# Tensor sums and low parts moved from the Pool engine to VectorE in the last three stages of a decoder block

## The chip, the cores and the metric

One core of a Trainium2 chip runs the whole kernel. Its engines work side by side, each through its own list of instructions in order: TensorE (PE in the views) multiplies matrices, VectorE (DVE) and the Pool engine (POOL, GpSimd) do elementwise work, ScalarE (ACT) copies, casts and activations, and SyncE (SP) issues the DMAs. The metric is the device time of one execution, in microseconds, as the median over runs.

## The reference, cut to what matters

A decoder block on 1024 tokens (1152 rows with padding and meta tokens), width 1024, everything float32. Two attention branches are merged, projected and added to the residual; a SwiGLU feed-forward of width D_FF = 2816 follows:

```
mixed = gate_a * (o_a @ w_branch_a) + gate_b * (o_b @ w_branch_b)
h = h + mixed @ w_out                                  # 1024 x 1024 by 1024 x 1024
hn = rms_norm(h, ffn_norm_g)
h = h + (silu(hn @ w_ffn_gate) * (hn @ w_ffn_up)) @ w_ffn_down
y = rms_norm(h, final_norm_g)
```

## The kernel before, in words

**Products of float32 values in two parts.** Each operand is split into a high part, a rounded copy that ScalarE makes, and a low part, the difference of the raw value and the high one, which VectorE or POOL subtracts. A product is three matmuls: high by high, low by high, high by low (`mm3`, whose instructions stand at L193). So for every operand tile of 128 x 512 there is one cast, one subtraction ("the low") and then matmuls that wait for both.

**Seven products for eight.** The output projection, the feed-forward products and the down projection are Winograd's form of Strassen's method: a 2 x 2 block product takes the seven products m1 to m7, whose operands are blocks or sums of blocks: s1 to s4 of one side, t1 to t4 of the other. In the output projection and the down projection they come in the orders m1 m5 m6 m3 m2 m7 m4 and m1 m5 m6 m3 m7 m2 m4. Between a product and the next, an elementwise engine makes the sums in place.

**Three stages matter here.**

- The *output projection* (`winograd`, called by `phase_mix`). X is the merged attention output, W is `w_out`, four tiles of 128 x 512 for each block. x sums (L1188) and x lows (L133, tile `fhl`) are VectorE's; w sums (L1188 too) and w lows (L131, tile `tl`) are POOL's. `NTH = 5` buffers hold w parts. Where a product ends, VectorE adds it to `h1` (L1218); when a block of 128 tokens is whole, `row_scale` (L1240 to L1246, chains of 128 x 1 instructions), ScalarE's scaling `xs` (L1255), eight transposes (L1264) and the gain (L1267, tile `hb`) make the normed, transposed operand B.
- The *first feed-forward pair*. `phase_ffn` makes the sums t1 to t4 of B in four cuts of 128 tokens (L1289 to L1292, tiles `bt` and `hb`): POOL has t1 and t2 of the first cut and every t3 and t4, VectorE the others. `operand` (L1318, L1319) splits each of the seven operands of B once, in four tiles: three lows on VectorE, the fourth on POOL. `ffn_hidden(ap, q)` runs for q = 0 to 10, each q a pair of 128-column slices of D_FF; `weight` takes the gate and up weights' high part on ScalarE (L1360) and low part on POOL (L1361). Only q = 0 waits for the operands of B to be made; the later ones find them ready.
- The *down projection* (`ffn_down`). For each product there are eleven k steps of one activation tile `da` and one weight tile `wd`. The activation's low is VectorE's, the weight's low is POOL's (both L1432, tiles `fhl` and `yhl`; in the last product `xl` and `yl`); the sum of weight tiles (L1462 in m5, L1464 in m6, L1466 in m7, L1468 in m4) is POOL's where k is odd and VectorE's where it is even.

**What sets the order.** A list scheduler with a model of the engines puts each engine's instructions in order when the program is built; the code's order decides only where that model is indifferent. Within an engine the order then is fixed: an instruction that waits holds all behind it.

Of the kernel before, what the change touches and what calls it, by code (L numbers as in the profile page):

```python
# [7 lines left out]
F32 = mybir.dt.float32  # L8
# [95 lines left out]
class Program:  # L104
# [1028 lines left out]
    def phase_mix(self):  # L1133
        nc, I = self.nc, self.I

        self.act_dram = {nm: [self.dr.tile([P, 512], F32, name=f"act{nm}_{k}") for k in range(NF // 2)]
                         for nm in ("11", "12", "22", "s1", "s2", "s3", "s4")}
        self.h1_dram = [self.dr.tile([P, D], F32, name=f"h1_dram{b}") for b in range(NB)]
        self.f_es, mes = ExitStack(), ExitStack()
        self.B, self.xs = {}, {}  # L1140
        self.fwp = self.f_es.enter_context(self.pool("fwp"))
        xp = mes.enter_context(self.pool("mixed"))

        X, W = self.X, self.W = [{ij: xp.tile([P, 4, 512], F32, name=f"{nm}{ij}") for ij in ("11", "12", "21", "22")} for nm in "xw"]
# [12 lines left out]
        for b in range(NB):
            with self.tc.issue_after(self.mixed_in):
                nc.sync.dma_start(self.h1[:, b, :], I["x"][0][P * b:P * b + P, :])
        self.rp = mes.enter_context(self.pool("ring", side="right"))  # L1160

        def done(b, nh):
            self.squares(b, nh)
            if nh == 0:
                nc.sync.dma_start(self.h1_dram[b], self.h1[:, b, :])
                self.norm_scaled(b)
                self.pending.append(b)
                if len(self.pending) > 1:
                    self.norm_transposed(self.pending.pop(0))

        self.pending = []
        banks = lambda name: [(self.sp if name in ("m2", "m5") else self.mm).tile(
            [P, 512], F32, name="s" if name in ("m2", "m5") else "ps", tag="s" if name in ("m2", "m5") else "ps") for _ in range(4)]
        self.winograd(X, W, 4, ("m1", "m5", "m6", "m3", "m2", "m7", "m4"), banks, nc.vector, nc.gpsimd, done)
        while self.pending:
            self.norm_transposed(self.pending.pop(0))
        mes.close()

    def winograd(self, a, b, kc, order, banks, seng, teng, done=None):

        nc = self.nc
        a, b, sums = dict(a), dict(b), {}

        def combine(eng, d, name, dst, x, y, op):
            for k in range(kc):
                eng.tensor_tensor(d[dst][:, k], d[x][:, k], d[y][:, k], op=op)  # L1188
            d[name] = d[dst]

        sub, plus = ALU.subtract, ALU.add
        for at, name in enumerate(order):
            if name == "m5":
                combine(seng, a, "s1", "21", "21", "22", plus)
                combine(teng, b, "t1", "12", "12", "11", sub)
            elif name == "m6":
                combine(seng, a, "s2", "s1", "s1", "11", sub)
                combine(teng, b, "t2", "t1", "22", "t1", sub)
            elif name == "m3":
                combine(seng, a, "s3", "11", "22", "s2", sub)  # L1200
                combine(teng, b, "t3", "11", "t2", "11", sub)
                combine(seng, a, "s4", "s2", "12", "s2", sub)
                combine(teng, b, "t4", "t2", "t2", "21", sub)
            an, bn, old, to = WINOGRAD[name]
            ps4 = sums[name] = sums[old] if old else banks(name)
            ops = []
            rows = name == "m4" and done
            for k in range(kc):
                ops.append((self.parts(a[an][:, k], self.fwp, ("fhl",), 4, False), self.parts(b[bn][:, k], self.rp, ("th", "tl"), NTH, True)))
            for k, i in [(k, i) for i in range(4) for k in range(kc)] if rows else [(k, i) for k in range(kc) for i in range(4)]:  # L1210
                c = slice(P * i, P * i + P)
                x, y = ops[k]
                self.mm3(ps4[i], [(x[0][:, c], x[1][:, c], *y)], start=not old and k == 0, stop=k == kc - 1, skip_group_check=bool(old))
                if k < kc - 1:
                    continue
# [54 lines left out]
    def phase_ffn(self):  # L1270
# [14 lines left out]
        B["t3"] = B["12"]  # L1285
        for at, n in CUTS:
            cut = {nm: B[nm][:, :, at:at + n] for nm in B}
            e = nc.gpsimd if at < 128 else nc.vector
            e.tensor_sub(cut["t1"], cut["12"], cut["11"])  # L1289
            e.tensor_sub(cut["t2"], cut["22"], cut["t1"])  # L1290
            nc.gpsimd.tensor_sub(cut["t3"], cut["22"], cut["12"])
            nc.gpsimd.tensor_sub(cut["t4"], cut["21"], cut["t2"])  # L1292
        self.tp2 = tp
        self.ring = es.enter_context(self.pool("dring"))
        with self.pool("act") as ap:
# [14 lines left out]
    def operand(self, name):  # L1310

        nc, hi = self.nc, self.Bhi[name]
        if name not in self.Blo:
# [2 lines left out]
            lo = self.Blo[name] = pool.tile([P, 4, 512], F32R, name=f"l{name}", tag=tag, bufs=1)  # L1316
            for k in range(4):
                nc.scalar.copy(hi[:, k], raw[:, k])  # L1318
                (nc.gpsimd if k == 3 else nc.vector).tensor_sub(lo[:, k], raw[:, k], hi[:, k].bitcast(F32))  # L1319
        return hi, self.Blo[name]  # L1320

    def parts(self, src, ring, tags, bufs, lo_pool):
# [9 lines left out]
    def ffn_hidden(self, ap, q):  # L1332
# [12 lines left out]
        def weight(a, name):  # L1345
# [74 lines left out]
    def ffn_down(self):  # L1420
# [6 lines left out]
        homes = {"11": ("h11", "h21", "b11"), "12": ("ht2", "b21", "ht1"), "22": ("bt2", "ht3", "bt1"), "21": ("h22", "b12", "ht4")}  # L1427
        rings, turn = ("bt4", "spare"), 0

        def split(src, hi, lo, pool):  # L1430
            nc.scalar.copy(hi, src)  # L1431
            (nc.gpsimd if pool else nc.vector).tensor_sub(lo, src, hi.bitcast(F32))  # L1432

        sums, gain = {}, None
        for name in ("m1", "m5", "m6", "m3", "m7", "m2", "m4"):
# [8 lines left out]
            for g, (k0, n) in enumerate(groups):  # L1444
# [8 lines left out]
                for i in range(n):  # L1453
# [3 lines left out]
                    if fresh:  # L1457
                        r, c = P * (2 * k + int(fresh[0]) - 1), 512 * (int(fresh[1]) - 1)
                        dma = nc.sync.dma_start(b[fresh][k], wd[r:r + P, c:c + 512])
                    e = nc.gpsimd if k % 2 else nc.vector  # L1460
                    if name == "m5":
                        e.tensor_sub(b["12"][k], b["12"][k], b["11"][k])  # L1462
                    elif name == "m6":
# [86 lines left out]
```

## Time and profile before

| | us |
|---|---|
| median of 3 runs | 1518.8 (1517.16 to 1520.61) |
| the profiled execution: time | 1516.53 |
| its span on the core | 1514.8 |
| TensorE busy, share of the span | 1398.1 (92%) |
| VectorE busy | 1009.9 (67%) |
| POOL busy | 914.7 (60%) |
| ScalarE busy | 817.0 (54%) |

The profiled execution has 1.7 us around its span and is 2.3 us under the median. Times in the views count from the start of the span. The output projection runs from about 744 to 832 us, the first feed-forward pair to about 913, the other ten pairs to about 1280, the down projection and the final norm to the end. Windows of the trace give busy time per engine in such a stretch; the timeline gives single instructions with the idle time in front and what ended it; the chain of waits is followed back from the last instruction.

### The profile page before, as it was taken

What the parts mean: (1) busy time and instruction counts of PE and PEld (TensorE: products, weight loads), DVE (VectorE), ACT (ScalarE), POOL (GpSimd) and SP (SyncE); (2) the same over time, 40 slices, a digit from 0 to 9 for tenths busy, and PEclk for the clock granted to TensorE, in tenths of its full rate; (3) what the DMA queues carried; (4) which work ended last, traced back from release to release, by engine and by line L of the source; (5) the groups of instructions that cost most, each with busy time, mean ns of one, the idle gap of its engine ahead of it and who ended that gap; (6) DMA issues with size and microseconds to landing.
All of it is one profiled execution on the core that took longest, in us unless ns stands there. A gap on an engine that the chain in (4) does not pass through costs nothing.

```text
span 1514.8 us, 21375 instructions
## 1 busy us (share of the span) xinstructions
PE 1398.1 (92%) x6847; PEld 1160.4 (77%) x6847; DVE 1009.9 (67%) x1950; ACT 817.0 (54%) x1743; POOL 914.7 (60%) x995
## 2 busy tenths in 40 slices
PE   4999697898898899999989699999999999999997
PEld 4988685677677688888768478888888888878876
DVE  7268997135686887785798984444444446697576
ACT  6347585983787777885336533333333334434463
POOL 4147465667665657664794675555555557596575
PEclk9999898999899899999999699999999999999999
DMA  6421121246444755337812023332232239723332
GB/s 207 133 77 29 29 71 49 91 138 198 125 138 126 182 147 162 125 102 236 308 54 94 18 97 126 106 109 96 100 104 97 99 105 317 295 70 121 115 105 111
DMA packets 148038, 189.79 MB, mean 125 GB/s; under 512 B 11331, under 2 KB 95126, under 8 KB 147670
## 3 DMA queue, kind: packets, MB, share of 16 engines
q1 hardware_dynamic: 147568, 188.28, 38.6%
q8 instruction: 54, 0.88, 0.2%
q14 instruction: 58, 0.48, 0.1%
q10 hardware_dynamic: 198, 0.14, 0.0%
q0 software_dynamic: 160, 0.01, 0.0%
HBM read 133.49 MB, written 58.03 MB: 126 GB/s over the span
## 4 chain that ended last, share of the span: by engine, by line
PE 60%; DVE 15%; POOL 7%; issue 7%; ACT 6%; DMA 6%; SPq 1%; POOLq 0%; ACTq 0%; DVEq 0%
PE ps L193 24%; PE s L193 20%; PE gps L193 8%; DVE mask L815 4%; ACT mask L857 2%; PE pv L1049 2%; PE s L1007 2%; PE tp L1038 2%; DMA kraw<-bk_dram 1%; DMA ga<-gate_dram 1%; POOL yhl L1432 1%; POOL y L1511 1%; PE tp L198 1%; PE pv L193 1%; DVE fhl L1432 1%
## 5 line engine op out<-in xcount | busy, mean ns | idle before, releaser
L1361 POOL TENSOR_TENSOR fhl<-fs,fhl 128x512 fp32r<-128x512 f32 x88 | 120.7, 1394 | 98.1 <-ACT fhl L1360 98.1
L1361 POOL TENSOR_TENSOR fhl<-fr,fhl 128x512 fp32r<-128x512 f32 x66 | 105.6, 1621 | 84.4 <-ACT fhl L1360 72.6
L188 POOL TENSOR_TENSOR w_lo<-w_raw,w_hi 128x512 fp32r<-128x512 f32 x60 | 82.4, 1375 | 90.5 <-ACT w_hi L187 76.3
L1432 POOL TENSOR_TENSOR yhl<-wd,yhl 128x512 fp32r<-128x512 f32 x66 | 96.5, 1468 | 55.2 <-ACT yhl L1431 53.6
L193 PE MATMUL s<-ht,fhl 128*128 128x512 f32 x384 | 123.4, 396 | 2.0 <-ACT fhl L1360 2.0
L1432 DVE TENSOR_TENSOR fhl<-da,fhl 128x512 fp32r<-128x512 f32 x66 | 89.2, 1365 | 47.0 <-ACT fhl L1431 46.8
L193 PE MATMUL ps<-ht,fhl 128*128 128x512 f32 x320 | 101.1, 392 | 0.0
L193 PE MATMUL gps<-oh,w_hi 128*128 128x512 f32 x232 | 94.6, 408 | 6.7 <-ACT gt L914 6.1
L857 ACT ACTIVATE mask<-high,smallg 128x784 bf16<-128x784 uint16 (+3 forms) x66 | 70.4, 1067 | 45.9 <-POOL smallg L866 28.1
L193 PE MATMUL s<-yhl,fhl 128*128 128x512 f32 x396 | 92.6, 392 | 2.5 <-POOL yhl L1432 2.3
L865 POOL TENSOR_SCALAR smallg<-smallg 128x1 f32<-128x1 f32 x128 | 58.8, 462 | 59.8 <-ACT mask L857 59.3
L193 PE MATMUL ps<-yhl,fhl 128*128 128x512 f32 x396 | 92.1, 391 | 1.5 <-DVE fhl L1432 1.5
L193 PE MATMUL gps<-ol,w_hi 128*128 128x512 f32 x232 | 93.4, 403 | 0.0
L193 PE MATMUL gps<-oh,w_lo 128*128 128x512 f32 x232 | 92.6, 399 | 0.0
L1431 ACT CAST yhl<-wd 128x512 fp32r<-128x512 f32 x66 | 41.0, 621 | 95.0 <-PE ps L193 43.2
L193 PEld LDWEIGHTS s<-yhl,fhl 128*128 128x128 f32 x396 | 74.0, 188 | 20.3 <-POOL yhl L1432 4.5
L193 PEld LDWEIGHTS ps<-yhl,fhl 128*128 128x128 f32 x396 | 74.0, 188 | 18.9 <-DVE fhl L1432 3.1
L193 PE MATMUL s<-h,fhl 128*128 128x512 f32 x272 | 88.2, 395 | 0.0
L193 PE MATMUL ps<-h,fhl 128*128 128x512 f32 x256 | 84.8, 403 | 3.6 <-ACT h L1318 3.6
L193 PEld LDWEIGHTS s<-ht,fhl 128*128 128x128 f32 x384 | 72.8, 190 | 19.4 <-ACT fhl L1360 2.8
L133 DVE TENSOR_TENSOR ptl<-tp,pth 128x512 fp32r<-128x512 f32 (+2 forms) x112 | 70.9, 645 | 24.2 <-ACT pth L127 22.9
L1360 ACT CAST fhl<-fr 128x512 fp32r<-128x512 f32 x66 | 39.7, 619 | 73.9 <-issue 33.3
(486 smaller groups left out, 4459.5 us busy)
## 6 DMA issues: line engine op xcount, KB each, us to landing
fr<-in_w_ffn_gate SPq DMA_DIRECT2D x22, 512.0 KB, 4.0
fr<-in_w_ffn_up SPq DMA_DIRECT2D x22, 512.0 KB, 4.7
wd<-in_w_ffn_down SPq DMA_DIRECT2D x44, 256.0 KB, 5.1
da<-acts SPq DMA_DIRECT2D x44, 256.0 KB, 3.9
w_raw<-in_w_in SPq DMA_DIRECT2D x40, 256.0 KB, 3.1
act<-a SPq DMA_DIRECT2D x33, 256.0 KB, 2.1
da<-act SPq DMA_DIRECT2D x33, 256.0 KB, 3.0
acts<-s SPq DMA_DIRECT2D x33, 256.0 KB, 2.0
```

Of the source, the lines that this page charges most:

```text
L133: nc.vector.tensor_sub(lo, ps, hi.bitcast(F32))
L188: (nc.vector if lo_dve else nc.gpsimd).tensor_sub(t[1], t[2], t[0].bitcast(F32))
L193: mm = self.nc.tensor.matmul(*args, **kw)
L815: nc.vector.tensor_scalar(self.mask[j], src[j], at[:, i:i + 1], None, op0=op, op1=ALU.add, accum_out=out[:, i:i + 1])
L857: nc.scalar.activation(self.mask[j], src[j], AF.Sign, bias=at[:, i:i + 1], scale=scale, accum_out=out[:, i:i + 1])
L865: g.tensor_scalar(c[:, o], acc[:, o], bar[:, o], b[:, o], op0=ALU.is_ge, op1=ALU.subtract)
L1007: nc.tensor.matmul(ps[:, :n], q[k][:, h, qc:qc + P], kb[:, h, at:at + n], start=k == 0, stop=k == 1)
L1038: mm = nc.tensor.transpose(pt[:, P * i:P * i + P], prs[par, e][:, NM + P * rr:NM + P * rr + P], self.ident)
L1360: nc.scalar.copy(hi, a[name])
L1361: nc.gpsimd.tensor_sub(lo, a[name], hi.bitcast(F32))
L1431: nc.scalar.copy(hi, src)
L1432: (nc.gpsimd if pool else nc.vector).tensor_sub(lo, src, hi.bitcast(F32))
```

## The change

The diff takes POOL out of 172 subtractions and sums: 28 w lows and 16 w sums of the output projection, the ten sums of B's cuts that POOL had, the fourth low of each of the seven operands, the 14 weight lows of q = 0, and in the down projection 77 weight lows and 20 weight sums. All go to VectorE in the same shape. POOL keeps the 140 weight lows of q = 1 to 10 and its work in the final norm. No cast, matmul or DMA is added or removed.

```diff
-        self.winograd(X, W, 4, ("m1", "m5", "m6", "m3", "m2", "m7", "m4"), banks, nc.vector, nc.gpsimd, done)
+        self.winograd(X, W, 4, ("m1", "m5", "m6", "m3", "m2", "m7", "m4"), banks, done)
...
-        def combine(eng, d, name, dst, x, y, op):
+        def combine(d, name, dst, x, y, op):
             for k in range(kc):
-                eng.tensor_tensor(d[dst][:, k], d[x][:, k], d[y][:, k], op=op)
+                nc.vector.tensor_tensor(d[dst][:, k], d[x][:, k], d[y][:, k], op=op)
             d[name] = d[dst]
...
             if name == "m5":
-                combine(seng, a, "s1", "21", "21", "22", plus)
-                combine(teng, b, "t1", "12", "12", "11", sub)
+                combine(a, "s1", "21", "21", "22", plus)
+                combine(b, "t1", "12", "12", "11", sub)
...
-                ops.append((self.parts(a[an][:, k], self.fwp, ("fhl",), 4, False), self.parts(b[bn][:, k], self.rp, ("th", "tl"), NTH, True)))
+                ops.append((self.parts(a[an][:, k], self.fwp, ("fhl",), 4, False), self.parts(b[bn][:, k], self.rp, ("th", "tl"), NTH, False)))
...
-            e = nc.gpsimd if at < 128 else nc.vector
-            e.tensor_sub(cut["t1"], cut["12"], cut["11"])
-            e.tensor_sub(cut["t2"], cut["22"], cut["t1"])
-            nc.gpsimd.tensor_sub(cut["t3"], cut["22"], cut["12"])
-            nc.gpsimd.tensor_sub(cut["t4"], cut["21"], cut["t2"])
+            nc.vector.tensor_sub(cut["t1"], cut["12"], cut["11"])
+            nc.vector.tensor_sub(cut["t2"], cut["22"], cut["t1"])
+            nc.vector.tensor_sub(cut["t3"], cut["22"], cut["12"])
+            nc.vector.tensor_sub(cut["t4"], cut["21"], cut["t2"])
...
-                (nc.gpsimd if k == 3 else nc.vector).tensor_sub(lo[:, k], raw[:, k], hi[:, k].bitcast(F32))
+                nc.vector.tensor_sub(lo[:, k], raw[:, k], hi[:, k].bitcast(F32))
...
-            nc.gpsimd.tensor_sub(lo, a[name], hi.bitcast(F32))
+            (nc.gpsimd if q else nc.vector).tensor_sub(lo, a[name], hi.bitcast(F32))
...
-            (nc.gpsimd if pool else nc.vector).tensor_sub(lo, src, hi.bitcast(F32))
+            nc.vector.tensor_sub(lo, src, hi.bitcast(F32))
...
-                    e = nc.gpsimd if k % 2 else nc.vector
+                    e = nc.vector
```

The new engine also changes what the scheduler puts beside what. From L1289 on, the changed file's line numbers are one lower.

VectorE, where the output projection goes over to m5, in the kernel before: x lows (`fhl`), sums of the x blocks (`x_8542` and `x_8540` are the blocks 21 and 11).

```order
L1188 TENSOR_TENSOR x_8542<-x_8542,x_8543 128x512
L133 TENSOR_TENSOR fhl<-x_8542,fhl 128x512
L1188 TENSOR_TENSOR x_8542<-x_8542,x_8540 128x512
L1188 TENSOR_TENSOR x_8540<-x_8543,x_8542 128x512
L133 TENSOR_TENSOR fhl<-x_8542,fhl 128x512
```

The same place in the changed kernel, from the last merge (L1117) on; `tl` are the w lows, `w_8545` and `w_8544` w blocks.

```order
L1117 TENSOR_TENSOR x_8542<-gt,ga 128x512
L1188 TENSOR_TENSOR x_8542<-x_8542,x_8543 128x512
L133 TENSOR_TENSOR tl<-w_8544,th 128x512 x4
L133 TENSOR_TENSOR tl<-w_8545,th 128x512
L1188 TENSOR_TENSOR w_8545<-w_8547,w_8545 128x512
L1188 TENSOR_TENSOR w_8544<-w_8545,w_8544 128x512
L133 TENSOR_TENSOR fhl<-x_8542,fhl 128x512
L133 TENSOR_TENSOR tl<-w_8545,th 128x512
L1188 TENSOR_TENSOR x_8542<-x_8542,x_8540 128x512
L1188 TENSOR_TENSOR w_8545<-w_8547,w_8545 128x512
L1188 TENSOR_TENSOR x_8540<-x_8543,x_8542 128x512
L1188 TENSOR_TENSOR w_8544<-w_8545,w_8544 128x512
```

Each k step of VectorE's list has grown from three instructions to six, and the first four w lows stand behind the last merge.

VectorE, where the sums of B's cuts (`bt`, `hb` of L1289 and L1290) lead to the first operands that need them, in the kernel before; L1267 is the gain on the transposed norm.

```order
L1289 TENSOR_TENSOR bt_9649<-hb_8781,hb_8779 128x4x128
L1267 TENSOR_TENSOR hb_8782<-s,vec 128x4x128
L1289 TENSOR_TENSOR bt_9649<-hb_8781,hb_8779 128x4x128
L1290 TENSOR_TENSOR bt_9650<-hb_8782,bt_9649 128x4x128 x2
L1319 TENSOR_TENSOR l_9742<-hb_8780,h_9653 128x512 x3
L1357 TENSOR_TENSOR fs<-fr,fs 128x512
```

And in the changed kernel, where L1288 to L1291 are t1 to t4, L1318 is the operand's low and L1360 a weight low:

```order
L1267 TENSOR_TENSOR hb_8782<-s,vec 128x4x128
L1290 TENSOR_TENSOR hb_8781<-hb_8782,hb_8781 128x4x128
L1288 TENSOR_TENSOR bt_9649<-hb_8781,hb_8779 128x4x128 x2
L1291 TENSOR_TENSOR bt_9651<-hb_8780,bt_9650 128x4x128
L1360 TENSOR_TENSOR fhl<-fs,fhl 128x512
L1289 TENSOR_TENSOR bt_9650<-hb_8782,bt_9649 128x4x128
L1290 TENSOR_TENSOR hb_8781<-hb_8782,hb_8781 128x4x128
L1289 TENSOR_TENSOR bt_9650<-hb_8782,bt_9649 128x4x128
L1290 TENSOR_TENSOR hb_8781<-hb_8782,hb_8781 128x4x128
L1318 TENSOR_TENSOR l_9742<-hb_8780,h_9653 128x512 x4
```

Between the last gain and the operand's lows there are now nine instructions of VectorE where there were three, and four lows where there were three.

VectorE in the down projection, before, at m5 beside the sums that m6 will want (`wd` the weight tiles, `fhl<-da` the activation lows):

```order
L1466 TENSOR_TENSOR wd_1_12858<-wd_1_13104,wd_1_12858 128x512
L1432 TENSOR_TENSOR fhl<-da,fhl 128x512 x2
L1464 TENSOR_TENSOR wd_2_13142<-wd_2_13383,wd_2_13142 128x512
L1466 TENSOR_TENSOR wd_2_12892<-wd_2_13142,wd_2_12892 128x512
L1432 TENSOR_TENSOR fhl<-da,fhl 128x512 x2
```

And after:

```order
L1431 TENSOR_TENSOR fhl<-da,fhl 128x512
L1465 TENSOR_TENSOR wd_0_12824<-wd_0_13066,wd_0_12824 128x512
L1463 TENSOR_TENSOR wd_1_13104<-wd_1_13345,wd_1_13104 128x512
L1431 TENSOR_TENSOR yhl<-wd_1_13104,yhl 128x512
L1431 TENSOR_TENSOR fhl<-da,fhl 128x512
L1465 TENSOR_TENSOR wd_1_12858<-wd_1_13104,wd_1_12858 128x512
```

Each k step is now four instructions on VectorE (L1463, two lows, L1465); before, VectorE had four for two steps, and POOL did the other four beside it.

## Rows read from the trace of the kernel before

**Rows 1.** The page: busy time of each engine over the span, and the shares of the chain that ended last.

```profile
PE 1398.1 (92%) x6847; PEld 1160.4 (77%) x6847; DVE 1009.9 (67%) x1950; ACT 817.0 (54%) x1743; POOL 914.7 (60%) x995
...
PE 60%; DVE 15%; POOL 7%; issue 7%; ACT 6%; DMA 6%; SPq 1%; POOLq 0%; ACTq 0%; DVEq 0%
```

**Rows 2.** Windows: start and end, length, then busy time and number of instructions of PE, PEld, DVE, ACT and POOL, the granted clock of TensorE, the DMA share and GB/s.

```profile
743.60:784.00 40.40, 35.68 (x148) 27.18 (x147) 39.44 (x33) 14.31 (x26) 40.33 (x24) 1.00 0.48 176
784.00:832.10 48.10, 47.76 (x221) 38.57 (x221) 41.85 (x91) 28.20 (x61) 26.05 (x18) 1.00 0.16 66
832.10:857.90 25.80, 15.69 (x60) 11.88 (x58) 25.59 (x51) 13.36 (x23) 16.34 (x13) 0.67 0.10 42
857.90:884.00 26.10, 20.14 (x73) 15.36 (x73) 23.36 (x21) 15.25 (x29) 20.04 (x13) 0.87 0.07 23
884.00:912.80 28.80, 28.80 (x118) 23.40 (x119) 23.55 (x24) 9.66 (x18) 19.43 (x13) 0.94 0.38 127
912.80:1280.00 367.20, 367.20 (x1600) 300.23 (x1599) 178.59 (x210) 129.27 (x233) 201.67 (x139) 1.00 0.36 122
1280.00:1318.00 38.00, 38.00 (x168) 31.07 (x167) 23.79 (x26) 15.42 (x27) 19.05 (x14) 1.00 0.94 344
1318.00:1350.60 32.60, 31.66 (x134) 24.51 (x133) 32.46 (x24) 12.56 (x22) 32.22 (x20) 1.00 0.19 62
1350.60:1383.50 32.90, 31.35 (x134) 24.37 (x132) 32.11 (x26) 12.56 (x22) 27.94 (x18) 1.00 0.35 116
1383.50:1443.40 59.90, 59.90 (x266) 49.64 (x265) 33.20 (x32) 27.47 (x52) 30.09 (x23) 1.00 0.31 106
1443.40:1467.00 23.60, 22.04 (x98) 17.94 (x97) 16.68 (x20) 17.68 (x36) 18.15 (x13) 1.00 0.24 79
```

**Rows 3.** The timeline of PE around the output projection's start and the first feed-forward pair: start, length, what, and in brackets the idle time in front and what ended it.

```profile
743.59 1.09 PE L193 MATMUL ps<-th,fhl 128*128 128x512 f32 x4
745.51 0.51 PE L193 MATMUL ps<-tl,fhl 128*128 128x512 f32 x1 [0.83 <-POOL tl L131]
...
832.12 0.39 PE L193 MATMUL ps<-th,fhl 128*128 128x512 f32 x1
836.09 1.22 PE L193 MATMUL ps<-h,fhl 128*128 128x512 f32 x2 [3.58 <-ACT h L1318]
840.35 1.97 PE L1264 MATMUL s<-ident,xs 128*128 128x128 f32 x8 [3.04 <-ACT xs L1255]
...
860.82 0.79 PE L193 MATMUL ps<-l,fhl 128*128 128x512 f32 x1 [2.94 <-DVE l L1319]
...
883.99 0.80 PE L193 MATMUL s<-ht,fhl 128*128 128x512 f32 x1 [0.89 <-ACT fhl L1360]
```

**Rows 4.** The timeline of VectorE at the end of the last feed-forward pair, with POOL at rest.

```profile
1286.79 0.69 DVE L1411 TENSOR_TENSOR s<-a,a 128x512 f32<-128x512 f32 x1
1287.51 0.69 DVE L1412 TENSOR_TENSOR s<-s,a 128x512 f32<-128x512 f32 x1
1288.12 0.68 DVE L1413 TENSOR_TENSOR a<-a,a 128x512 f32<-128x512 f32 x1
1288.72 0.69 DVE L1432 TENSOR_TENSOR fhl<-da,fhl 128x512 fp32r<-128x512 f32 x1
```

**Rows 5.** The timeline of POOL in the down projection's m1, with VectorE at rest beside it.

```profile
1299.89 1.30 POOL L1432 TENSOR_TENSOR yhl<-wd,yhl 128x512 fp32r<-128x512 f32 x1 [1.47 <-ACT yhl L1431]
```

**Rows 6.** The timeline of all engines in the down projection's m5.

```profile
1329.96 1.79 DVE L1464 TENSOR_TENSOR wd<-wd,wd 128x512 f32<-128x512 f32 x1
...
1331.29 1.63 POOL L1464 TENSOR_TENSOR wd<-wd,wd 128x512 f32<-128x512 f32 x1
1331.79 1.68 DVE L1466 TENSOR_TENSOR wd<-wd,wd 128x512 f32<-128x512 f32 x1
...
1332.88 1.75 POOL L1432 TENSOR_TENSOR yhl<-wd,yhl 128x512 fp32r<-128x512 f32 x1
```

**Rows 7.** The timeline of all engines at the end of the output projection, where the norm's small instructions meet POOL's weight lows of q = 0.

```profile
831.34 3.74 POOL L1361 TENSOR_TENSOR fhl<-fr,fhl 128x512 fp32r<-128x512 f32 x3 [11.85 <-DVE rh L1245]
831.35 1.30 DVE L1246 SCALAR_TENSOR_TENSOR rh<-rh 128x1 f32<-128x1 f32 x1
...
832.57 2.52 DVE L1245 SCALAR_TENSOR_TENSOR rh<-rh 128x1 f32<-128x1 f32 x2
...
835.02 0.15 DVE L1246 SCALAR_TENSOR_TENSOR rh<-rh 128x1 f32<-128x1 f32 x1
```

**Rows 8.** Groups of POOL's instructions from 740 to 1515 us, shapes kept apart: count, then busy time and mean ns of one, idle time in front and what ended it.

```profile
L1432 POOL TENSOR_TENSOR yhl<-wd,yhl 128x512 fp32r<-128x512 f32 x66 | 96.5, 1468 | 55.2 <-ACT yhl L1431 53.6 <-DMA wd<-in_w_ffn_down 1.4
L131 POOL TENSOR_TENSOR tl<-w,th 128x512 fp32r<-128x512 f32 x28 | 45.9, 1656 | 14.9 <-ACT th L127 10.2 <-PE tp L193 4.7
```

**Rows 9.** The chain of waits from 1316 to 1334 us, by line.

```profile
by line: POOL yhl L1432 44.6%; POOL wd L1464 27.1%; issue 27.1%; POOL wd L1466 11.0%; POOLq L1432 0.2%; POOLq L1464 0.1%
```

**Rows 10.** The timeline of VectorE at the start of the output projection.

```profile
744.96 1.05 DVE L1117 TENSOR_TENSOR x<-gt,ga 128x512 f32<-128x512 f32 x1
746.04 1.67 DVE L1188 TENSOR_TENSOR x<-x,x 128x512 f32<-128x512 f32 x1
```

**Rows 11.** Windows around the first feed-forward pair's idle stretches; the columns are those of rows 2.

```profile
836.10:853.10 17.00, 10.49 (x38) 8.29 (x39) 16.79 (x42) 6.70 (x9) 8.84 (x8) 0.50 0.08 31
860.00:866.80 6.80, 5.98 (x14) 4.73 (x15) 5.85 (x4) 5.66 (x11) 6.72 (x5) 0.50 0.01 2
```

More of the change, by code (lines that the diff above doesn't have):

```diff
@@ L1177, in phase_mix, with winograd @@
         mes.close()
-    def winograd(self, a, b, kc, order, banks, seng, teng, done=None):
+    def winograd(self, a, b, kc, order, banks, done=None):
         nc = self.nc
         a, b, sums = dict(a), dict(b), {}
-        def combine(eng, d, name, dst, x, y, op):
+        def combine(d, name, dst, x, y, op):
             for k in range(kc):
-                eng.tensor_tensor(d[dst][:, k], d[x][:, k], d[y][:, k], op=op)
+                nc.vector.tensor_tensor(d[dst][:, k], d[x][:, k], d[y][:, k], op=op)
             d[name] = d[dst]
@@ L1193, in winograd @@
             if name == "m5":
-                combine(seng, a, "s1", "21", "21", "22", plus)
-                combine(teng, b, "t1", "12", "12", "11", sub)
+                combine(a, "s1", "21", "21", "22", plus)
+                combine(b, "t1", "12", "12", "11", sub)
             elif name == "m6":
-                combine(seng, a, "s2", "s1", "s1", "11", sub)
-                combine(teng, b, "t2", "t1", "22", "t1", sub)
+                combine(a, "s2", "s1", "s1", "11", sub)
+                combine(b, "t2", "t1", "22", "t1", sub)
             elif name == "m3":
[L1200 to L1203, printed above, removed]
+                combine(a, "s3", "11", "22", "s2", sub)
+                combine(b, "t3", "11", "t2", "11", sub)
+                combine(a, "s4", "s2", "12", "s2", sub)
+                combine(b, "t4", "t2", "t2", "21", sub)
             an, bn, old, to = WINOGRAD[name]
@@ L1428, in ffn_down, with split @@
         rings, turn = ("bt4", "spare"), 0
-        def split(src, hi, lo, pool):
+        def split(src, hi, lo):
             nc.scalar.copy(hi, src)
-            (nc.gpsimd if pool else nc.vector).tensor_sub(lo, src, hi.bitcast(F32))
+            nc.vector.tensor_sub(lo, src, hi.bitcast(F32))
         sums, gain = {}, None
@@ L1475, in ffn_down @@
                         op = t[:, 0], t[:, 1], u[:, 0], u[:, 1]
-                    split(x, *op[:2], False)
-                    split(y, *op[2:], True)
+                    split(x, *op[:2])
+                    split(y, *op[2:])
                     ops.append(op)
```

## The prediction

> **What bounds the kernel now.** I first read the page: TensorE is busy for 92% of the span and holds 60% of the chain that ended last, so a change on VectorE and POOL can win only where TensorE stands still; VectorE has 15% of that chain and POOL 7% [rows 1]. Then the windows, to find those places. The rate without gaps is 59.90 us for 266 matmuls in 1383.5 to 1443.4, 0.225 us each [rows 2]. Against it:
>
> - start of the output projection, 743.6 to 784.0: 148 matmuls need 33.3 us and took 40.4, so 7.1 are lost; POOL is busy for 40.33 of these 40.4 and VectorE for 39.44;
> - end of the output projection to the third product of the first feed-forward pair, 832.1 to 884.0: 133 instructions of TensorE in 51.9 us, with VectorE busy for 25.59 + 23.36 = 48.95;
> - down projection: m5 (1318.0 to 1350.6) 134 x 0.225 = 30.2 of 32.6, lost 2.4; m6 (to 1383.5) 30.2 of 32.9, lost 2.7; m2 (1443.4 to 1467.0) 98 x 0.225 = 22.1 of 23.6, lost 1.5; together 6.6.
>
> From 912.8 to 1318.0 TensorE is busy all the time (367.20 of 367.20, 38.00 of 38.00) [rows 2].
>
> The PE timeline says who is late: POOL's `tl` at 745.51, after the output projection ScalarE's casts and `xs` (836.09, 840.35), which stand behind VectorE's norm, VectorE's `l` at 860.82 [rows 3]. In m5 the chain is POOL: 44.6% lows, 27.1% and 11.0% weight sums [rows 9].
>
> The timeline of VectorE and POOL then gives the reason. VectorE alone takes 0.68 us for a 128x512 subtraction of two SBUF tiles, and where one does not need the result before it the next starts 0.60 later (1287.51 to 1288.12, 1288.12 to 1288.72); where it does, 0.72 (1286.79 to 1287.51) [rows 4]. POOL alone takes 1.30 [rows 5]. When both work, each takes 1.63 to 1.79, and the starts on either engine lie 1.6 to 1.8 apart [rows 6]: a pair costs about 1.70, and two on VectorE alone would cost 1.20. POOL's help is worth less than nothing there. Even a 128x1 instruction of the norm takes 1.30 or 1.26 beside POOL (831.35, 832.57 for two) and 0.15 without it (835.02) [rows 7].
>
> **The change part by part.** It takes 172 instructions from POOL, whose mean is 1468 ns for `yhl` and 1656 ns for `tl` [rows 8], and gives 172 to VectorE; at 0.60 these are 103 us more. What decides is VectorE's pitch p in a mixed queue. Its bounds are 0.60 and 0.72 [rows 4]; I take 0.63, near the lower end, since the order puts other instructions between a sum and the low made from it, and a twentieth for the few that stand in a row. No cast, matmul or DMA is added.
>
> *A, start of the output projection.* The first w low, which POOL had made by 745.5, now stands behind the last merge (744.96) and a sum [rows 10, 3]. At 0.6 to 0.7 each VectorE comes to it at 746.3, and TensorE to the first `tl` at 746.9, 1.4 later than before. From there TensorE needs 144 matmuls x 0.225 = 32.4, to 779.3. VectorE has 52 instructions up to the first x low of m3: 31.2 us at 0.60 (777.5), 32.8 at 0.63 (779.0), 37.4 at 0.72 (783.7). TensorE sets the end in the first two. m3 began at 784.0: gain 4.7, 4.7 or 0.3. A w low now waits for its cast on VectorE, and behind it stand x sums and the `h1` additions that free PSUM banks. ScalarE is busy for only 14.31 of the 40.4 us [rows 2], so I cost that at nothing; were the casts late, POOL's 10.2 us of waiting for them [rows 8] would be the ceiling.
>
> *B, norm and first pair.* m3 to the end is bound by TensorE (47.76 of 48.10 [rows 2]) and moves along. Of the 32 transposes, 16 now stand behind m4's matmuls, which end some 1.8 us earlier for it (16 x 0.11; eight take 1.97 at half clock in rows 3, so half of that at the full one). m4 ends at 832.1 - 4.7 - 1.8 = 825.6. From there to the third product VectorE has 74 tile instructions and 35 small ones at some 0.13: 49.0 us at 0.60, 51.2 at 0.63, 57.9 at 0.72 (there from 830.0). The third product starts at 874.6, 876.8 or 887.9 instead of 884.0: gain of A and B together 9.4, 7.2 or -3.9. That VectorE takes 14 weight lows and 17 sums and operand lows here is why B gives little beyond A. What is late next is still VectorE. Afterwards TensorE is the bound as before, and POOL's 140 later lows are unchanged: 912.8 to 1280 moves as a block.
>
> *C, down projection.* In m5 VectorE has 48 instructions: 22 lows, 22 sums (those of m5 and m6) and 4 additions to `h1`. That is 28.8 us at 0.60, 30.2 at 0.63, 34.6 at 0.72, against 132 x 0.225 = 29.7 of TensorE. So m5 loses nothing, 0.6, or 4.4 to 4.9 (some 2 more than before); m6 and m2, with fewer sums left, lose nothing. Gain 6.6, 6.0 or 2.2. POOL was busy for 32.22 of 32.6 in m5 [rows 2]; its queue is now empty. m1 is bound by TensorE with the DMA engines at 0.94 [rows 2] and only moves; a weight sum that waits for its DMA now holds VectorE's other work, which I put at 0 to 2 us and take at 0, as TensorE had no gap there.
>
> Sum: -16.0 at 0.60, -13.2 at 0.63, +1.7 at 0.72. The profiled execution took 1516.53, so it would be 1503.3; the median lies 2.3 above, and 1518.8 - 13.2 = 1505.6 us.
>
> **The rivals.**
>
> *Each instruction waits until the one before is through.* Then p is 0.68, the duration itself [rows 4]. A: 52 x 0.68 = 35.4, to 781.7, gain 2.3. B: from 828.0, 74 x 0.68 + 4.6 = 54.9, to 882.9, gain of both 1.1. C: 48 x 0.68 = 32.6 in m5, as before; m6 and m2 give 4.2. Together -5.3: 1513.5. For it: dependent pairs do show 0.72. Against it: the starts 0.60 apart in rows 4. The Trainium skill, page "VectorE: DVE Perf Modes", section "The DRAIN you can't avoid", says this as a rule: the next operation doesn't start until the pipeline is empty, though it adds that one not held starts earlier. By that rule the time would be the 1513.5; the trace of rows 4 shows the exception as the common case.
>
> *Slower: VectorE becomes the bound.* One in-order queue for x lows, w lows, sums and `h1` additions; each low waits for its cast, and each wait holds the rest. If the mean pitch, waits included, is above 0.71 (between -5.3 at 0.68 and +1.7 at 0.72), the kernel is slower; at 0.72 1520.5, at 0.75 about 5 us more, 1526. For it: before, POOL waited 53.6 us for casts of `yhl` [rows 8], a wait that would now stand on VectorE. Against it: POOL waited mostly where it was ahead, as it was busy throughout m5, and ScalarE was busy for only 12.56 of 32.6 there.
>
> *The gain ahead of the feed-forward is taken back.* If something else than VectorE sets the start of the third product (weights' DMA, the cast on ScalarE, which released 836.09 and 883.99 [rows 3]), A and B give nothing and C's 6.0 stay: 1512.8. Against it: the DMA share there is 0.10 and 0.07, ScalarE at 13.36 of 25.8 and 15.25 of 26.1 [rows 2].
>
> *More than forecast.* TensorE ran at a granted clock of 0.50, 1.2 GHz, after its idle stretches, for 17.0 and 6.8 us [rows 11]. If shorter pauses keep it at 2.4 GHz, the 14 matmuls from 860 cost 14 x 0.225 = 3.2 us less; with p at 0.60 as well, -19: 1500.
>
> **How the numbers follow.** Forecast (p 0.60 to 0.65, 1502 to 1510) 0.56; more than that 0.12; a part only, by the 0.68 or by lost A and B (1510 to 1515.7) 0.15; no change 0.07; slower 0.10. What a measurement of this kernel can tell from no change is about 0.2%, 3 us. So faster 0.83, same 0.07, slower 0.10. The range 1498 to 1517 leaves out some 0.04 below and 0.14 above; it holds the ends 0.60 and 0.68, not 0.72.
>
> **What would show it.** Right: VectorE's tile subtractions at 0.68 long and 0.60 apart in the output projection and m5, none at 1.7; the norm's small instructions at 0.15 to 0.2; m3 at about 779 and the third product at about 877; TensorE without gaps in m5, m6 and m2. Wrong: tile instructions 0.68 to 0.72 apart, gaps on VectorE released by ScalarE's casts, TensorE waiting for `yhl` or `tl` from VectorE in more than the first microseconds of a product, or a third product that starts no earlier than 884.

## The result and the profile after

The changed kernel takes 1500.61 us (median of 4 runs, 1498.89 to 1501.66), the kernel before 1519.7 (4 runs, 1517.16 to 1521.56): ratio 0.9866, 95% interval 0.9847 to 0.9885, so 17 to 23 us faster. Forecast were 1505.6 and a range of 1498 to 1517. In a second series beside other kernels the ratio was 0.9873 (0.9847 to 0.9899). The two profiled executions took 1516.53 and 1500.29, 16.2 apart; the one of before lies below all four of its timed runs, which is why the medians lie further apart than the traces.

The page of the changed kernel, engines and chain, beside [rows 1]:

```profile
PE 1388.4 (93%) x6847; PEld 1157.7 (77%) x6847; DVE 990.8 (66%) x2122; ACT 818.1 (55%) x1743; POOL 648.8 (43%) x823
...
PE 64%; DVE 14%; issue 6%; ACT 6%; DMA 5%; POOL 5%; SPq 1%; POOLq 0%; ACTq 0%; DVEq 0%
```

VectorE has 172 instructions more and is busy for 19.1 us less. So a part of its busy time before was not its own work. Windows of the changed kernel, columns as in [rows 2], cut where its stages now begin:

```profile
744.20:781.40 37.20, 34.52 (x142) 27.36 (x141) 36.46 (x61) 13.88 (x25) 0.00 (x0) 0.95 0.51 189
781.40:829.30 47.90, 47.73 (x214) 38.43 (x213) 37.98 (x93) 28.13 (x58) 0.00 (x0) 1.00 0.13 51
829.30:855.80 26.50, 14.79 (x75) 11.82 (x73) 24.61 (x72) 14.07 (x26) 0.00 (x0) 0.74 0.17 68
855.80:878.30 22.50, 18.94 (x78) 14.25 (x78) 22.50 (x39) 17.31 (x31) 0.00 (x0) 1.00 0.14 43
878.30:904.30 26.00, 25.97 (x113) 21.17 (x114) 20.07 (x27) 7.87 (x14) 8.98 (x6) 1.00 0.37 126
904.30:1271.40 367.10, 367.10 (x1599) 299.95 (x1598) 184.99 (x217) 129.10 (x233) 194.66 (x134) 1.00 0.36 123
1309.20:1339.20 30.00, 30.00 (x134) 24.82 (x134) 29.14 (x49) 12.57 (x22) 0.00 (x0) 1.00 0.30 97
1339.20:1369.10 29.90, 29.90 (x134) 24.76 (x133) 22.48 (x37) 12.57 (x22) 0.00 (x0) 1.00 0.29 98
```

POOL does nothing in the output projection and in m5 and m6; TensorE has no idle time left in m5 and m6 (30.00 of 30.00, 29.90 of 29.90); VectorE is still nearly full from 744 to 781 and from 829 to 878 (36.46 of 37.20, 24.61 of 26.50, 22.50 of 22.50); between them TensorE is (47.73 of 47.90). The timeline of VectorE in the output projection, which answers to [rows 4, 6]:

```profile
752.97 0.68 DVE L133 TENSOR_TENSOR tl<-w,th 128x512 fp32r<-128x512 f32 x1
753.57 0.68 DVE L1188 TENSOR_TENSOR x<-x,x 128x512 f32<-128x512 f32 x1
754.18 0.68 DVE L1188 TENSOR_TENSOR w<-w,w 128x512 f32<-128x512 f32 x1
754.78 0.69 DVE L1188 TENSOR_TENSOR x<-x,x 128x512 f32<-128x512 f32 x1
```

Starts lie 0.60 apart, in lows and sums alike. PE's timeline, answering to [rows 3]:

```profile
744.23 1.09 PE L193 MATMUL ps<-th,fhl 128*128 128x512 f32 x4
747.99 0.70 PE L193 MATMUL ps<-tl,fhl 128*128 128x512 f32 x1 [2.68 <-DVE tl L133]
748.50 0.63 PE L193 MATMUL ps<-th,fhl 128*128 128x512 f32 x1
...
828.98 0.39 PE L193 MATMUL ps<-th,fhl 128*128 128x512 f32 x1
...
836.17 1.22 PE L193 MATMUL ps<-h,fhl 128*128 128x512 f32 x2 [5.05 <-ACT h L1317]
843.23 4.71 PE L1264 MATMUL s<-ident,xs 128*128 128x128 f32 x24 [5.83 <-ACT xs L1255]
...
859.07 0.50 PE L193 MATMUL ps<-l,fhl 128*128 128x512 f32 x1 [3.30 <-DVE l L1318]
```

The pauses around the norm are still there. Of the chain in m5 and m6 [rows 9] nothing is left but TensorE:

```profile
1309.41 29.92 PE s L193 x132
1339.33 29.92 PE ps L193 x132
```

Where the time went, by the starts of the same matmuls in PE's timeline: the first of the output projection (743.59 before, 744.23 after), the last of its m4 (832.12, 828.98), the first behind "to the second pair" (912.80, 904.26), the first of m5 (1317.98, 1309.25), m3 (1383.50, 1369.09), m2 (1443.34, 1428.93) and the end of the span. The matmul at 912.80 is not quite the second pair's first. A pair has seven products of 24 matmuls, and from the last of m4 to 912.80 TensorE does 216 matmuls, a whole pair and two products of the next, which begins at 901.80 (893.23 in the changed kernel). It is the same matmul in every run, so the differences stand, and "the second pair" means it from here on.

| stretch | before | changed | difference | forecast |
|---|---|---|---|---|
| output projection | 88.53 | 84.76 | -3.8 | -6.5 |
| to the second pair | 80.69 | 75.28 | -5.4 | -0.7 |
| to m5 | 405.18 | 404.99 | -0.2 | 0 |
| m5 and m6 | 65.51 | 59.84 | -5.7 | -4.5 |
| m3 and m7 | 59.84 | 59.84 | 0 | 0 |
| m2 to the end | 71.42 | 69.59 | -1.8 | -1.5 |
| all | 771.17 | 754.30 | -16.9 | -13.2 |

### The profile page after: what moved, and what is told of

Its sections match the earlier page's. It is cut to its first block, busy times and chain, and to the rows that moved or that the text cites. A ratio compares the mean times of both kernels' runs of the same rounds, so it can differ in the third digit from the quotient of the medians.

```text
span 1498.5 us, 21232 instructions
## 1 busy us (share of the span) xinstructions
PE 1388.4 (93%) x6847; PEld 1157.7 (77%) x6847; DVE 990.8 (66%) x2122; ACT 818.1 (55%) x1743; POOL 648.8 (43%) x823
## 4 chain that ended last, share of the span: by engine, by line
PE 64%; DVE 14%; issue 6%; ACT 6%; DMA 5%; POOL 5%; SPq 1%; POOLq 0%; ACTq 0%; DVEq 0%
PE ps L193 25%; PE s L193 23%; PE gps L193 7%; DVE mask L815 4%; ACT mask L857 2%; PE pv L1049 2%; PE s L1007 2%; PE tp L1038 2%; DMA ga<-gate_dram 1%; PE tp L198 1%; POOL y L1510 1%; PE pv L193 1%; DMA kraw<-bk_dram 1%; DMA wa_raw<-in_w_in 1%; DVE hb L1267 1%
## 5 line engine op out<-in xcount | busy, mean ns | idle before, releaser
L1360 POOL TENSOR_TENSOR fhl<-fr,fhl 128x512 fp32r<-128x512 f32 x60 | 97.5, 1645 | 223.0 <-ACT fhl L1359 223.0
L1360 POOL TENSOR_TENSOR fhl<-fs,fhl 128x512 fp32r<-128x512 f32 x80 | 106.5, 1355 | 106.8 <-ACT fhl L1359 106.8
L1430 ACT CAST yhl<-wd 128x512 fp32r<-128x512 f32 x66 | 41.1, 622 | 89.9 <-PE ps L193 50.2
L1431 DVE TENSOR_TENSOR yhl<-wd,yhl 128x512 fp32r<-128x512 f32 x66 | 45.6, 691 | 50.2 <-ACT yhl L1430 50.2
L193 PE MATMUL s<-lt,fhl 128*128 128x512 f32 x192 | 75.3, 392 | 0.0
```

Of the source, the lines that this page charges most:

```text
L193: mm = self.nc.tensor.matmul(*args, **kw)
L1360: (nc.gpsimd if q else nc.vector).tensor_sub(lo, a[name], hi.bitcast(F32))
L1431: nc.vector.tensor_sub(lo, src, hi.bitcast(F32))
```

## The experiments

My theory: VectorE and POOL, subtracting at once, hold each other, so that POOL's share costs VectorE more than it saves. Rivals: that the new order or a gain of one stage alone did it; that POOL was merely slow and late with its results; that VectorE's number of instructions is the bound. Stage times below are made as in the table. The phases ahead of the output projection vary between executions (its first matmul lay between 742.53 and 754.17 us in these profiles), so the stages tell more than the totals.

**The three parts alone.** Each is the kernel before with one part of the change: the output projection, the norm and first pair (with t3 and t4 of all cuts as well), the down projection.

```diff
-        self.winograd(X, W, 4, ("m1", "m5", "m6", "m3", "m2", "m7", "m4"), banks, nc.vector, nc.gpsimd, done)
+        self.winograd(X, W, 4, ("m1", "m5", "m6", "m3", "m2", "m7", "m4"), banks, nc.vector, nc.vector, done)
...
-                ops.append((self.parts(a[an][:, k], self.fwp, ("fhl",), 4, False), self.parts(b[bn][:, k], self.rp, ("th", "tl"), NTH, True)))
+                ops.append((self.parts(a[an][:, k], self.fwp, ("fhl",), 4, False), self.parts(b[bn][:, k], self.rp, ("th", "tl"), NTH, False)))
```

```diff
-            e = nc.gpsimd if at < 128 else nc.vector
+            e = nc.vector
...
-                (nc.gpsimd if k == 3 else nc.vector).tensor_sub(lo[:, k], raw[:, k], hi[:, k].bitcast(F32))
+                nc.vector.tensor_sub(lo[:, k], raw[:, k], hi[:, k].bitcast(F32))
...
-            nc.gpsimd.tensor_sub(lo, a[name], hi.bitcast(F32))
+            (nc.gpsimd if q else nc.vector).tensor_sub(lo, a[name], hi.bitcast(F32))
```

```diff
-                    e = nc.gpsimd if k % 2 else nc.vector
+                    e = nc.vector
...
-                    split(y, *op[2:], True)
+                    split(y, *op[2:], False)
```

> Only the output projection's 28 w lows and 16 w sums go to VectorE; the rest is as before. If the gain comes from VectorE and POOL no longer slowing each other, VectorE's tile instructions here are 0.60 apart, m3 starts some 2 to 3 us earlier against m1's start, and the time is 2 to 5 us under before. If VectorE's queue is the bound here (the rival on which the slower case rests), m3 starts no earlier and the time is that of before or above.

Measured: ratio 0.9981 (0.9967 to 0.9995), 1 to 5 us. Output projection 84.70 (-3.8), the stretch behind it 81.61 (+0.9), the others within 0.7 of before.

> Only the ten sums of B, the seven fourth lows and the 14 weight lows of q = 0 go to VectorE. Contention: the stretch from the last matmul of m4 to the start of the second feed-forward pair shrinks by 4 to 7 us and the time by as much. Rival, that this stretch is bound by VectorE's number of instructions and only what is ahead of it was won: 0, or up to 3 us slower, as VectorE has 31 instructions more at 0.60 (18.6 us).

Measured: 0.9959 (0.9943 to 0.9975). The stretch from m4 to the second pair takes 72.75 (-7.9), all else within 0.2 of before. It is shorter than in the full change (75.28), where 16 more transposes lie behind m4, and with them four more gains and ten more small instructions of VectorE.

> Only the down projection's 77 weight lows and 20 weight sums go to VectorE. Contention: m5 and m6 take 59.8 us together as in the changed kernel (65.7 before), the end moves 1.5 to 2 us more, in all 7 to 8 us under before. Rival, that the gain there needed the earlier changes (another order, an earlier start of the loads): under 3 us.

Measured: 0.9956 (0.9936 to 0.9976). m5 and m6 take 59.84 (-5.7), m2 to the end 69.61 (-1.8): to 0.02 us what the full change gives there.

So each part pays for itself. The first two add up to -10.9 over their two stretches alone and to -9.2 together, probably since they meet in one VectorE queue (no run tests this); the third is independent. The order made for the other stages isn't needed for any of it.

**The first product's w lows back on POOL.**

```diff
-                ops.append((self.parts(a[an][:, k], self.fwp, ("fhl",), 4, False), self.parts(b[bn][:, k], self.rp, ("th", "tl"), NTH, False)))
+                ops.append((self.parts(a[an][:, k], self.fwp, ("fhl",), 4, False), self.parts(b[bn][:, k], self.rp, ("th", "tl"), NTH, name == "m1")))
```

> The changed kernel, with the first product's four w lows put back on POOL. If the first tl was late because it stood behind the merges on VectorE (747.99 instead of 745.5, and 1.2 GHz until 751), TensorE reaches it 1.5 to 2.5 us earlier, the half clock goes too, and the time is 2 to 3.5 us under the changed kernel's 1500.6. Rival: the four subtractions and the merges slow each other and nothing is won, 0 to 1 us slower.

Measured: 0.9882 (0.9861 to 0.9903), no better than the change; the output projection takes 84.68 against 84.76. The first `tl` did come 2.2 us earlier, seen from the first matmul (746.76 - 745.19 against 747.99 - 744.23), and the lower clock behind it was gone (1.00 granted from 746.7 to 751.0). The timelines of PE, of POOL and of VectorE show why it bought nothing:

```profile
746.76 0.51 PE L193 MATMUL ps<-tl,fhl 128*128 128x512 f32 x1 [0.49 <-POOL tl L131]
```

```profile
745.26 6.56 POOL L131 TENSOR_TENSOR tl<-w,th 128x512 fp32r<-128x512 f32 x4 [6.27 <-ACT th L127]
```

```profile
749.00 1.68 DVE L1188 TENSOR_TENSOR x<-x,x 128x512 f32<-128x512 f32 x1
750.59 1.78 DVE L133 TENSOR_TENSOR tl<-w,th 128x512 fp32r<-128x512 f32 x1
```

Four subtractions on POOL took 6.56 us and stretched what VectorE ran beside them to 1.7; VectorE lost about what the four would have cost it. TensorE, ahead of the changed kernel by then, waited in m3 for VectorE's additions to `h1` and had a granted clock of 0.57 behind the wait, as PE's timeline and the window from 793 to 797 us show:

```profile
793.12 0.77 PE L193 MATMUL s<-th,fhl 128*128 128x512 f32 x1 [2.40 <-DVE h L1218]
```

```profile
793.00:797.00 4.00, 3.88 (x10) 3.14 (x11) 2.97 (x5) 2.58 (x8) 0.00 (x0) 0.57 0.02 4
```

In the changed kernel the wait at that place is 0.17 us. My expectation was wrong: the late first `tl` costs the stage next to nothing, since VectorE is hardly ahead of the late TensorE. Without the delay TensorE waits for it in m3, and pays the pause and the lower clock there.

**Work on POOL that nobody waits for.** The changed kernel with a tile that lands behind `h1` in m1, and 18 subtractions, or 36 fills, of it on POOL.

```diff
-                        nc.sync.dma_start(self.h1[:, t, :], self.h1_dram[t])
+                        dma = nc.sync.dma_start(self.h1[:, t, :], self.h1_dram[t])
+                d = self.fwp.tile([P, D], F32, name="dum", tag="fs", bufs=2)
+                with self.tc.issue_after(dma.ins):
+                    nc.sync.dma_start(d[:, :512], self.h1_dram[0][:, :512])
+                for _ in range(18):
+                    nc.gpsimd.tensor_sub(d[:, 512:], d[:, :512], d[:, :512])
```

For the fills, the last two lines are

```diff
+                for _ in range(36):
+                    nc.gpsimd.memset(d[:, :512], 0.0)
```

> The changed kernel, with 18 subtractions of 128x512 on POOL that nobody waits for, reading a tile of their own that lands with h1 in m1 (work added, the output is the same). If POOL holds VectorE, each costs a VectorE instruction 1.1 us: 20 us more on VectorE, of which m5's and m6's slack takes 8 to 12: m5 and m6 grow from 59.8 us by 5 to 19 us. Rival, that POOL was only late with its own results: nothing changes, 0 to 1 us.

Measured: 0.9947 (0.9928 to 0.9966). m5 and m6 take 72.11, that is 12.3 us more, and no other stretch changes by more than 0.1. POOL's timeline, then VectorE's:

```profile
1310.10 25.63 POOL L1486 TENSOR_TENSOR dum<-dum 128x512 f32<-128x512 f32 x18 [34.65 <-DMA dum<-h_dram]
```

```profile
1314.83 0.67 DVE L1500 TENSOR_TENSOR h<-h,ps 128x512 f32<-128x512 f32 x1
1315.43 0.93 DVE L1431 TENSOR_TENSOR fhl<-da,fhl 128x512 fp32r<-128x512 f32 x1
1316.28 1.27 DVE L1500 TENSOR_TENSOR h<-h,ps 128x512 f32<-128x512 f32 x2
...
1318.84 1.52 DVE L1431 TENSOR_TENSOR yhl<-wd,yhl 128x512 fp32r<-128x512 f32 x1
1320.29 1.52 DVE L1431 TENSOR_TENSOR fhl<-da,fhl 128x512 fp32r<-128x512 f32 x1
1321.73 1.52 DVE L1465 TENSOR_TENSOR wd<-wd,wd 128x512 f32<-128x512 f32 x1
...
1336.20 0.68 DVE L1431 TENSOR_TENSOR yhl<-wd,yhl 128x512 fp32r<-128x512 f32 x1
```

While POOL subtracts, VectorE's instructions on two SBUF tiles come to start 1.45 apart, one for each of POOL's (from 1318.84 on without a break); at 1336.20, behind POOL's last, they are at 0.68 again. The additions with one operand in PSUM (`h<-h,ps`, where `ps` is a bank that TensorE accumulates in) stay at 0.60 to 0.67 in the midst of it.

> The same kernel as with the 18 subtractions, but 36 fills of the same tile on POOL, which write and read nothing. If what holds VectorE is POOL reading SBUF, VectorE's instructions stay at 0.60 and m5 and m6 at 59.8 us. If any work of POOL holds it, they grow as with the subtractions.

Measured: 0.9883 (0.9858 to 0.9909); m5 and m6 take 59.84. The fills do run in m5, as POOL's timeline shows, and VectorE's group of activation lows from 1305 to 1370 us keeps its mean of 684 ns (868 over 19 of them with the subtractions):

```profile
1306.36 20.97 POOL L1486 MEMSET dum<- 128x512 f32 x36 [34.34 <-DMA dum<-h_dram]
```

```profile
L1431 DVE TENSOR_TENSOR fhl<-da,fhl 128x512 fp32r<-128x512 f32 x25 | 17.1, 684 | 0.5 <-ACT fhl L1430 0.5
```

The orders of TensorE, VectorE and ScalarE in these two kernels are the same, and neither's extra work has a reader. So what holds VectorE, where it works on two SBUF tiles, is POOL's subtracting and not its filling, and POOL's lateness is not needed for it. The subtractions read SBUF and the fills only write it; that the reading is what counts, and not the arithmetic, no run here separates. The Trainium skill, page "SBUF — State Buffer", section "Who interferes with whom", names the reading: a VectorE instruction with two SBUF inputs contends with a GpSimd instruction that reads SBUF, not with one that only writes. The trace agrees: VectorE's starts lie 1.45 apart beside the subtractions, 0.60 beside the fills. POOL's mere slowness does not explain m5 before either: its 20 instructions there [rows 2] would take 26.0 us at the 1.30 of one alone [rows 5], an estimate, and TensorE needs 29.9 for the product.

**The weight lows of q = 0 back on POOL.**

```diff
-            (nc.gpsimd if q else nc.vector).tensor_sub(lo, a[name], hi.bitcast(F32))
+            nc.gpsimd.tensor_sub(lo, a[name], hi.bitcast(F32))
```

> The changed kernel, with the 14 weight lows of q = 0 back on POOL. Between the end of m4 and the second feed-forward pair VectorE is busy nearly all the time, at 0.60 per instruction. If a POOL subtraction holds one of VectorE's for about 1.1 us more, each costs 1.1 and saves 0.60: that stretch grows by 1 to 7 us and the time with it. Rival, VectorE is the bound by its number of instructions alone: 14 x 0.60 = 8.4 less, so 2 to 8 us faster.

Measured: 0.9917 (0.9892 to 0.9942); m4 to the second pair takes 79.57, 4.3 more than in the changed kernel. The size was as expected; the way was so only in part. POOL's timeline, VectorE's and PE's:

```profile
875.52 10.87 POOL L1360 TENSOR_TENSOR fhl<-fs,fhl 128x512 fp32r<-128x512 f32 x4 [4.28 <-ACT fhl L1359]
```

```profile
874.71 2.48 DVE L1318 TENSOR_TENSOR lt<-hb,ht 128x512 fp32r<-128x512 f32 x4
877.12 0.68 DVE L1353 TENSOR_TENSOR fs<-fr 128x512 f32<-128x512 f32 x1
877.72 2.49 DVE L1318 TENSOR_TENSOR l<-hb,h 128x512 fp32r<-128x512 f32 x4
```

```profile
881.39 1.22 PE L193 MATMUL s<-ht,fhl 128*128 128x512 f32 x2 [3.46 <-POOL fhl L1360]
```

Here it is POOL that is held: VectorE runs nine lows and sums at 0.60 without a break, and POOL, which started at 875.52, is not through with its first subtraction until 881.3 (5.82 us in the chain of waits); TensorE waits 3.46 for it. Behind its run VectorE is held too: its next four lows, from 880.24 on, take 6.70 us.

**All other weight lows on VectorE too.**

```diff
-            (nc.gpsimd if q else nc.vector).tensor_sub(lo, a[name], hi.bitcast(F32))
+            nc.vector.tensor_sub(lo, a[name], hi.bitcast(F32))
```

> The changed kernel, with the other 140 weight lows (q = 1 to 10) on VectorE too. TensorE had no gap from 912.8 to 1280, so by the account so far the time stays within 1.5 us of the changed kernel, and VectorE is busy for some 84 us (140 x 0.60) more, less what the contention took. Rival, the longer queue of VectorE makes TensorE wait for weights: gaps in the feed-forward, over 3 us slower.

Measured: 0.991 (0.9881 to 0.9938), not told apart from the 0.9883 (0.9858 to 0.9909) of the fills on the same chip; by the medians it is 3.8 us above them, more than the 1.5 expected. From the first matmul of the output projection on, its trace is 1.1 us longer than the changed kernel's (755.37 against 754.30). The window that answers to 904.30 to 1271.40 above:

```profile
909.60:1276.70 367.10, 367.10 (x1599) 299.76 (x1598) 221.26 (x351) 129.49 (x233) 0.00 (x0) 1.00 0.36 122
```

TensorE has no gap there, as before; VectorE's busy time grew by 36 us (221.26 against 184.99) for 134 instructions more, which at 0.60 are 80 us, so the contention had cost it some 44. Contention here, where TensorE is the bound, costs the kernel nothing. m4 to the second pair took 1.5 us more in another order (76.79), which I did not follow up.

**Fewer instructions on VectorE.** Here the gain multiplications of the norm go to ScalarE, half of them (kh = 1) or all.

```diff
-            nc.vector.tensor_mul(dst[:, :, P * (b % 4):P * (b % 4) + P], pt.rearrange("p (k t) -> p k t", k=4),
-                                 g.unsqueeze(2).to_broadcast([P, 4, P]))
+            if kh:
+                for k in range(4):
+                    nc.scalar.activation(dst[:, k, P * (b % 4):P * (b % 4) + P], pt[:, P * k:P * k + P], AF.Copy, scale=g[:, k:k + 1])
+            else:
+                nc.vector.tensor_mul(dst[:, :, P * (b % 4):P * (b % 4) + P], pt.rearrange("p (k t) -> p k t", k=4),
+                                     g.unsqueeze(2).to_broadcast([P, 4, P]))
```

For all of them the condition is `if True`.

> The changed kernel, with 8 of the norm's 16 gain multiplications (kh = 1) taken by ScalarE, as four 128x128 activations each, in place of VectorE. If VectorE's count at 0.60 sets the stretch from m4 to the third product, 8 x 0.60 = 4.8 us go, and 3 to 5 us of it reach the end. Rival, that the norm's chain (squares, row_scale, xs, transposes) sets it and VectorE only fills the time: 0, or some us slower, as ScalarE gets 32 activations in front of its casts.

Measured: 0.9851 (0.9828 to 0.9874), beside 0.9873 for the changed kernel on the same chip. m4 to the second pair takes 71.91 against 75.46 there, -3.5. The stage gain is plain, the intervals of the whole overlap.

> The same with all 16 on ScalarE: 9.6 us less on VectorE, 64 activations more on ScalarE (8 to 16 us). If VectorE alone is the bound, 5 to 8 us faster than the changed kernel; if ScalarE takes its place, no better than with half of them.

Measured: 0.9894 (0.9875 to 0.9912); the stretch takes 77.53. PE's timeline shows the new bound:

```profile
845.07 4.04 PE L1264 MATMUL s<-ident,xs 128*128 128x128 f32 x16 [8.57 <-ACT xs L1255]
854.38 4.04 PE L1264 MATMUL s<-ident,xs 128*128 128x128 f32 x16 [4.56 <-ACT xs L1255]
```

TensorE waits 8.57 and 4.56 for ScalarE's `xs`, and ScalarE is busy for 24.60 of the 24.60 us from 833.4 to 858.0. With half moved, VectorE's count was the bound and 3.5 of 4.8 us came through; with all, ScalarE's queue is.

> The changed kernel unchanged, beside the two that follow and on the same chip: 1500 to 1505 us, 0.983 to 0.990 of before.

Measured: 1501.06 us, 0.9873 (0.9847 to 0.9899). Its stretches repeat those of the first profile to 0.7 us.

## Why the prediction was right, and where it was off

- *What bounds the kernel.* Right. The places where TensorE stood still were the two stages and m5, m6, m2, and all of the gain lies there; the long stretch from the second pair to m5 moved as a block (-0.2).
- *The reason.* Right, and shown by runs for m5 and m6: 18 subtractions that nobody waits for put 12.3 us back, 36 fills nothing. For the output projection and the norm it rests on the pitch, 0.60 where it was 1.6 to 1.8, and on the parts alone, which each gained.
- *The pitch p.* The term that was mis-sized. I took 0.63 with a twentieth for dependent pairs; the changed trace shows 0.60 nearly throughout (in the output projection's first 37 us five of 59 neighbours lie 0.72 or 0.73 apart, elsewhere hardly any). At 0.60 the working gave -16.0, and the traces differ by 16.2. That this is so close is in part luck: of the stretches, the first gave 2.7 less than forecast and the second 4.7 more.
- *C.* Forecast -6.0, measured -7.5: at 0.60 the 48 instructions of VectorE fit into m5 (29.14 busy of 30.00), so the 0.6 of loss that I had left there wasn't. Every gap in m5, m6 and m2 closed, and they were larger than the working had them: 5.7 in m5 and m6, where I had 5.1 because I took the windows' 134 matmuls for a product's 132, and 1.8 in m2 and behind, where I had 1.5.
- *A.* The weakest step. Forecast -4.7 and 1.8 for the transposes, measured -3.8 in all; m3 begins at 781.4 instead of 779. I had put the first `tl` at 3.3 us behind the first matmul; it came at 3.8, and behind the 2.68 us of waiting TensorE had a granted clock of 0.53, near its lower level of 1.2 GHz. I had not priced that, though [rows 11] show it behind pauses:

```profile
747.90:751.10 3.20, 3.11 (x8) 2.43 (x9) 3.14 (x6) 0.00 (x0) 0.00 (x0) 0.53 1.10 357
```

  Eight matmuls there start 0.43 apart instead of 0.23, some 1.6 us more; with the 0.5 of the later `tl` that is most of the 2.7 that are missing. Behind it TensorE's longest wait in the output projection is 0.17:

```profile
793.85 0.47 PE L193 MATMUL s<-th,fhl 128*128 128x512 f32 x1 [0.17 <-DVE h L1218]
```

  So "TensorE sets the end" held. But the run with POOL's four lows shows that VectorE is right behind: with an earlier `tl` TensorE runs into it in m3, and the stage is no shorter.
- *B.* Forecast -0.7 for the stretch, measured -5.4. The prediction's point 884.0 is not where the third product starts; that is 868.75, and by 884.0 TensorE is in the fifth. Behind 884.0 TensorE does not wait any more; in the changed kernel the like point is 878.33. PE's timeline of before:

```profile
868.75 0.63 PE L193 MATMUL s<-ht,fhl 128*128 128x512 f32 x2
```

  From the last of m4 up to that point it is 51.9 before and 49.4 in the changed kernel, 2.5 of the 5.4. The working has 51.2 there at 0.63 and 49.0 at 0.60, so some 2.2 are the pitch (74 x 0.03). From there on it is 28.8 and 25.9, where the working had no change. The changed kernel has 112 matmuls left instead of 118, some 1.4 us, and the other 1.5 are the clock: before, eight of them ran at a granted 0.50, and the changed kernel has 1.00 from 855.8 to 904.3. A window of before:

```profile
883.90:887.30 3.40, 3.31 (x8) 2.64 (x9) 3.37 (x3) 2.05 (x5) 2.21 (x2) 0.50 0.69 224
```

  That last part belongs to the rival "more than forecast".
- *The rivals.* The slower one fell: VectorE did become the bound from 829 to 878, as it says, and nearly so before 793, but at 0.60, far from the 0.71 from which that would have cost time. VectorE waits 50.2 us for casts of `yhl` (53.6 on POOL before [rows 8]), and none of it reached TensorE:

```profile
L1431 DVE TENSOR_TENSOR yhl<-wd,yhl 128x512 fp32r<-128x512 f32 x66 | 45.6, 691 | 50.2 <-ACT yhl L1430 50.2
```

  The rule of the drain (page "VectorE: DVE Perf Modes" of the Trainium skill, "The DRAIN you can't avoid") would have given starts 0.68 apart; here the next one, not held, starts at 0.60, as the same section allows. That the gain ahead of the feed-forward would be taken back did not happen.

## What to carry to other kernels

Before two elementwise engines share a stage, look at their rows side by side: where both show stretched durations at the same time, the second engine may cost more than it brings, and the comparison is the pair's pace against twice the faster engine's own. Read that pace as the distance between starts, not as durations, and without a margin where the trace shows none. Where a new order makes TensorE wait, price the lower clock behind the wait too. Take work off the shared path first where TensorE waits, leave it where TensorE is full, and compare stages by the same matmul, since phases ahead can move a whole run by more than one part of the edit does.

## What had not been expected

- Both can be the one that is held. POOL working back to back paces VectorE at 1.45; VectorE in a run of nine at 0.60 holds one subtraction of POOL for 5.82 us; alone one takes 1.30 [rows 5].
- POOL's fills beside VectorE cost nothing (59.84 us for m5 and m6 with 36 of them), and VectorE's additions with a PSUM operand kept 0.60 to 0.67 beside POOL's subtractions.
- The start of the output projection varied by 11.6 us over thirteen profiles. Where only the down projection was changed it lay at 754.17, 10.6 later than in the kernel before. What moves it was not settled.
